# Feed-forwards in chunks of 4, 8, 6 and 4 inner tiles instead of 4, 6, 6 and 6

## The chip, the cores and the metric

The kernel runs on one core of one Trainium2 chip. A core has a matrix engine (TensorE, "PE" in the profile; its weight loads are listed apart as "PEld"), a vector engine (VectorE, "DVE"), a scalar engine (ScalarE, "ACT"), a general one (GpSimd, "POOL") and a queue engine (SyncE, "SP"), each with its own instruction stream, and DMA queues that move data between DRAM and the on-chip memory. The engines run side by side and wait for each other through semaphores. The metric is device time in microseconds for one execution; lower is better. The time of a kernel is the median of several executions.

## The reference

The model is a two-layer decoder trunk over 528 tokens (16 meta tokens and 512) of width 1024 in float32. Each layer has a feed-forward, a token mixer, and a second feed-forward, each between two RMS norms, with a residual:

```python
def swiglu(x, w_in, w_out):
    gate, up = jnp.split(x @ w_in, 2, axis=-1)
    return (jax.nn.silu(gate) * up) @ w_out

for layer in range(DEPTH):
    g = norm_gains[layer]
    h = h + 0.5 * rmsnorm(swiglu(rmsnorm(h, g[0]), w_ffn_in[layer, 0], w_ffn_out[layer, 0]), g[1])
    hn = rmsnorm(h, g[2])
    ...
    h = h + rmsnorm(mix, g[3])
    h = h + 0.5 * rmsnorm(swiglu(rmsnorm(h, g[4]), w_ffn_in[layer, 1], w_ffn_out[layer, 1]), g[5])
    if layer == N_A_LAYERS - 1:
        k_sh, v_sh = shared_kv(h, kv_norm, w_kv, cos, sin)
return h[:, N_META:]
```

The mixer of layer 0 is chunked gated linear attention, that of layer 1 sliding-window attention over keys and values that are made once between the layers. The feed-forward's inner width is 2816, that is 22 tiles of 128. All weights come from DRAM.

## The kernel before

Activations lie transposed: 128 features on the partitions, tokens along the free dimension, so a token group of 272, 256 or 512 columns is the moving side of a matmul. Each float32 product is made of three matmuls on two float32r halves, high x high, low x high and high x low (`mm3`, L428; its instructions are all recorded at L202). So every weight tile that arrives from DRAM in a `raw` buffer is split before its use: ACT copies the high half (L271 for plain weights, L291 for half-size ones) and DVE subtracts it to get the low half (L274, L292). The two halves lie in one slot of a pool of 40 `pair` tiles.

A feed-forward (`ffn`, L876) goes through its 22 inner tiles in four chunks, `FF_CHUNKS` (L24).

- Chunk 0 is plain. Gate and up products of four inner tiles, then a plain down-projection whose result Y goes to DRAM as `y_sum` (`keep=True`).
- The others use a Strassen-Winograd scheme: a block product of two by two blocks is done in seven half-size products instead of eight. The profile shows these as `a`, `c`, `d` and `e`, by the PSUM bank they go to. One `Gated` item (L1120) makes gate and up of one inner tile: seven products of 4 x 3 matmuls each, 264 columns in layer 0, 256 in layer 1. The order of an item's products on PE is "11", "s1", "s2", "12", "s3", "s4", "22", but "11" of the next item is issued ahead of the last two of this one. Two `Gated` items fill one `Step` (L1046), whose seven combinations are the right-hand operands of a half-size down-projection. `Down` items (L1181), four for each of chunks 1 and 2, multiply them with the down weights: seven products of `nk` x 3 matmuls, with `nk` = 3 steps. Their result is added to `y_sum` in DRAM by POOL's DMA (L1213).
- The `Down` items of a chunk stand after the first `Gated` item of the next chunk (`BEFORE_DOWN`, L37). The last chunk has no `Down`: its inner tiles are turned into plain hidden tiles `hid` (L1173, ACT; L1174, DVE), and a plain down-projection (`out_steps`, L775) ends the feed-forward. It adds its products to Y (L816), which has been read back from `y_sum`.

In that last plain down-projection PE runs `y_m` for the eight output tiles m over token group 0, then the same over group 1; each `y_m` is 3 matmuls for each inner tile of the last chunk. Before the last hidden tile exists, PE begins `y_0`, `y_1` and `y_2` with the earlier hidden tiles (L844 to L847), `y_0` ahead of the last item's last products, the other two behind them. Each finished Y tile is squared (ACT, L534), summed (POOL, L535) and scaled (ACT, L835). After a group's last tile, `Residual.run` (L612) makes the norm's factor: PE sums the squares over the partitions (`st_post`), DVE does ten small operations (L446 to L460) and spreads the result on a diagonal (`dg_post`, L493), PE turns it into a row for all partitions (`r_post`). Then, for each of eight tiles, DVE adds to the residual H (L626, L627) and the next phase's operand is built: its high half on ACT (L564), its low half on DVE (L565). The next phase (`x` in the profile: `l0m` is layer 0's mixer, `kv` the shared keys and values, `l1m` layer 1's mixer) runs over group 0 first. After the last feed-forward there is no next phase; for group 1 `turn` (L649) sums the squares (`st_out`), transposes H and Y and writes the output.

PE's instructions stand in the order in which the program is written out; a planned clock (`Flow`, L77) decides at which point of that order the background jobs (splits, factors, builds) issue theirs. On DVE, ACT and POOL a scheduler orders them, and each engine works through its own list in order. The number of split half-size weights in flight is limited by `set_ahead(16, RING)` with ten slots.

The DVE operations of a half-size weight pair are sums of its quarters: a pair is either `summed`, where two of the sums are made by accumulating DMAs of POOL (L350), or in `plain_sums`, where DVE makes them (L324). Down weights with 384 columns were always the second kind.

Of the kernel before, what the change touches and what calls it, by code (L numbers as in the profile page):

```python
# [16 lines left out]
P = 128  # L17
D = 1024
KD = 8
# [3 lines left out]
NFF = 22  # L23
FF_CHUNKS = [(0, 4), (4, 10), (10, 16), (16, 22)]  # L24
LAST = 16
NLAST = NFF - LAST
# [6 lines left out]
RAWS = 13  # L33
RING = 10
STEP = 1.1
CHAINS = 2
BEFORE_DOWN = 1  # L37
# [103 lines left out]
def trunk_kernel(ctx: ExitStack, tc, a, out, last_out):  # L141
# [76 lines left out]
    units, plain_sums = [], set()  # L218
    for layer in range(2):
        for f in range(2):  # L220
            for ci, (lo, hi) in enumerate(FF_CHUNKS):
                for t in range(lo, hi):
# [4 lines left out]
                    if ci > 1 and t == lo + BEFORE_DOWN - 1:  # L227
                        units += [[a["w_down"][layer, f, ci - 2, m], a["w_down"][layer, f, ci - 2, m + 1]] for m in range(0, KD, 2)]
                if lo == 0:
# [104 lines left out]
    def load_unit():  # L334
        i = len(loaded)
        asked[0] += costs[i]
        owed[i] = costs[i]
        if isinstance(units[i], list):
            g, u = units[i]
            chains[0] += 1  # L340
            m = g.shape[-1] // 2
            summed = i not in plain_sums and m == 512
            a11, a12, a21, a22 = (b[:, c : c + m] for b in (g, u) for c in (0, m))
# [25 lines left out]
        else:  # L369
            n = units[i].shape[-1]  # L370
            raws = []
            for c in range(0, n, 512):
                m = min(512, n - c)
# [502 lines left out]
    def ffn(x, groups, finish, opening=False, tail=4):  # L876
# [62 lines left out]
        plan = []  # L939
# [4 lines left out]
        for c, (lo, hi) in enumerate(FF_CHUNKS[1:]):  # L944
            for t in range(hi - lo):
                plan.append(lambda c=c, t=t: Gated(tiles, steps[c][t // 2] if c < 2 else None, t % 2))
                if c and t == BEFORE_DOWN - 1:
                    plan += [lambda c=c, q=q: Down(tiles, steps[c - 1], q) for q in range(KD // 2)]
        lo, hi = FF_CHUNKS[-1]
        hids, jobs = [], []  # L950

# [8 lines left out]
        for i in range(len(plan)):  # L960
            last = i == len(plan) - 1
            if last:
                proj = out_steps(hids, groups, x.groups, False, finish, KD, True, jobs)
                end = used[0] + NLAST + tail
            cur.body((lambda: next(proj)) if last else (lambda: None))
            nxt = None if last else begin(plan[i + 1])
            job = cur.tail(last)
            if job is not None:
                jobs.append(job)
            cur = nxt  # L970
            if i == len(plan) - 4:
                Y.fresh()
                for q in range(KD // 2):
                    pool.dma_start(Y[:, 2 * q : 2 * q + 2, kept], y_sum[:, 2 * q : 2 * q + 2, kept])
# [206 lines left out]
    class Down(Item):  # L1181
        nk = 3

        def __init__(self, tiles, steps, q):
            super().__init__(tiles)
            self.steps, self.q = steps, q
            self.y = yp.tile([P, 2, TOK], F32, tag="dn", name=f"dn{self.name}")
# [636 lines left out]
def _layout(x, meta_tokens, norm_gains, w_ffn_in, w_ffn_out, gla_w_in, gla_w_gate, gla_b_gate, gla_norm,  # L1824
# [7 lines left out]
    c["w_out"] = wo[:, :, :, :, : FF_CHUNKS[0][1]].reshape(2, 2, KD, P, FF_CHUNKS[0][1] * P)  # L1832
    c["w_down"] = np.stack([
        np.concatenate([wo[:, :, :, :, lo + i : hi : 2] for i in range(2)], axis=4) for lo, hi in FF_CHUNKS[1:3]
    ], axis=2).reshape(2, 2, 2, KD, P, 6 * P)
    c["w_last"] = (
# [66 lines left out]
```

## Time and profile before

| | |
|---|---|
| median of 3 runs | 1846.03 us (1844.55 to 1847.69) |
| the profiled execution | 1848.01 us, span 1846.2, mean granted TensorE clock 0.997 |
| PE busy | 1834.5 us (99% of the span) in 14743 matmuls |
| DVE, ACT, POOL busy | 1459.9 (79%), 1119.6 (61%), 324.0 (18%) |
| half-size gated weights, DVE low half, 128x512 | 504 at 0.69 us each |
| the same of the down weights, 128x384 | 224 at 0.55 us each |
| sums of quarters on DVE, 128x384 | 128 at 0.55 us each |
| down results added in DRAM | 32 DMAs, 8.2 to 8.6 us from issue to landing |
| DMA | 270 MB moved, mean 146 GB/s |

The profile is one execution taken by the hardware profiler. The span is the time from the first to the last instruction; what the execution took beside it is 1.8 us. Busy times of PE count overlapping matmuls once. A row of a timeline has the start, the length, the engine, the line of the program, the operation, "output <- inputs" by the program's names, shapes and the number of instructions merged; in brackets stands the idle time before it and what ended it.

### The profile page before, as it was taken

To read this page: it belongs to the slowest core of one execution; us is meant where nothing else is said; L and a number is where in the kernel's file an instruction comes from. 1 tells how busy PE (TensorE), PEld (TensorE's weight loads), DVE (VectorE), ACT (ScalarE), POOL (GpSimd) and SP (SyncE) were. 2 spreads that over 40 slices of the span, in tenths; PEclk is the share of its full clock that TensorE was granted. 3 is DMA by queue.
4 is the path that set the end of the run, shared out by engine and by line. 5 is a ranking of instruction groups with operands and counts; after the bars stand their busy time and mean duration, and the time that the engine had idled before them with its cause. 6 is when DMAs were issued, how large, how long until landed. Compare 5 with 4: busy or idle time off the path is not lost.

```text
span 1846.2 us, 38789 instructions
## 1 busy us (share of the span) xinstructions
PE 1834.5 (99%) x14743; PEld 1780.8 (96%) x14743; DVE 1459.9 (79%) x3029; ACT 1119.6 (61%) x2613; POOL 324.0 (18%) x487
## 2 busy tenths in 40 slices
PE   9999999999999999999999999999999999999998
PEld 9999999999999999999999899999987898999998
DVE  6889888666664788988878789898667678898884
ACT  6666666654446566665665566666558765666564
POOL 2210101320001411011133110112320042111122
PEclk9999999999999999999999999999999999999999
DMA  6756659421213366666853565768421226657681
GB/s 244 196 152 156 166 150 247 151 70 58 69 58 115 105 173 154 155 167 151 252 180 104 143 161 148 181 151 243 153 80 47 70 91 162 161 152 175 156 252 49
DMA packets 143371, 269.98 MB, mean 146 GB/s; under 512 B 16080, under 2 KB 36432, under 8 KB 143184
## 3 DMA queue, kind: packets, MB, share of 16 engines
q1 hardware_dynamic: 113056, 194.94, 32.8%
q0 software_dynamic: 29696, 71.97, 19.6%
q8 instruction: 115, 1.88, 0.4%
q14 instruction: 72, 0.59, 0.1%
q10 hardware_dynamic: 432, 0.59, 0.1%
HBM read 230.74 MB, written 36.18 MB: 145 GB/s over the span
## 4 chain that ended last, share of the span: by engine, by line
PE 93%; DVE 4%; ACT 2%; issue 1%; DMA 1%; DVEq 0%; SPq 0%; POOLq 0%; ACTq 0%
PE a L202 28%; PE x L202 22%; PE y L202 17%; PE c L202 13%; PE d L202 7%; PE o L202 1%; DVE w L292 1%; PE po L202 1%; DVE w_s L292 1%; ACT s L1623 1%; DVE raw L297 1%; DMA raw<-in_w_in 1%; ACT w_s L291 0%; PE pt L214 0%; PE sa L202 0%
## 5 line engine op out<-in xcount | busy, mean ns | idle before, releaser
L292 DVE TENSOR_TENSOR w_s<-raw,w_s 128x512 fp32r<-128x512 f32 (+1 forms) x416 | 264.2, 646 | 73.6 <-ACT w_s L291 69.6
L291 ACT ACTIVATE w_s<-raw 128x512 fp32r<-128x512 f32 (+1 forms) x416 | 241.0, 592 | 89.2 <-DVE raw L324 49.2
L292 DVE TENSOR_TENSOR w<-raw,w 128x512 fp32r<-128x512 f32 (+1 forms) x312 | 196.2, 645 | 4.0
L274 DVE TENSOR_TENSOR w<-raw,w 128x512 fp32r<-128x512 f32 x248 | 164.5, 695 | 37.0 <-ACT w L271 34.7
L350 POOL DMA_DIRECT2D raw<-in_w_in x112 | 103.4, 967 | 453.2 <-DVE w L292 97.1
L291 ACT ACTIVATE w<-raw 128x512 fp32r<-128x512 f32 (+1 forms) x312 | 177.7, 589 | 0.0
L297 DVE TENSOR_TENSOR raw<-raw,raw 128x512 f32<-128x512 f32 (+1 forms) x256 | 162.7, 636 | 2.2
L202 PE MATMUL x<-x_l0m,w 128*128 128x272 f32 (+1 forms) x1152 | 152.2, 289 | 0.0
L202 PEld LDWEIGHTS x<-x_l0m,w 128*128 128x128 f32 x1152 | 143.4, 188 | 2.7 <-issue 1.7
L271 ACT ACTIVATE w<-raw 128x512 fp32r<-128x512 f32 x248 | 144.1, 620 | 2.5 <-DMA raw<-in_w_in 1.2
L535 POOL TENSOR_TENSOR acc_post<-acc_post,sq_post 128x256 f32<-128x256 f32 (+1 forms) x77 | 61.7, 802 | 360.8 <-ACT sq_post L534 357.2
L202 PE MATMUL y<-hidl0f,w 128*128 128x272 f32 (+1 forms) x960 | 119.3, 285 | 0.0
L202 PEld LDWEIGHTS y<-hidl0f,w 128*128 128x128 f32 x960 | 117.9, 188 | 0.2
L202 PE MATMUL a<-zl0f_t,w_s 128*128 128x264 f32 x864 | 116.8, 284 | 0.0
L202 PE MATMUL y<-hidl1f,w 128*128 128x256 f32 (+1 forms) x768 | 114.8, 310 | 0.0
L202 PE MATMUL a<-zl1f_t,w_s 128*128 128x256 f32 x864 | 113.8, 281 | 0.0
L202 PEld LDWEIGHTS y<-hidl1f,w 128*128 128x128 f32 x768 | 104.9, 188 | 8.5
L202 PEld LDWEIGHTS a<-zl0f_t,w_s 128*128 128x128 f32 x864 | 109.9, 188 | 0.0
L202 PEld LDWEIGHTS a<-zl1f_t,w_s 128*128 128x128 f32 x864 | 107.1, 188 | 0.0
L1213 POOL DMA_DIRECT2D kept_y<-dn x32 | 36.3, 1134 | 400.5 <-DVE w_s L292 203.7
L202 PE MATMUL x<-x_l0f,w 128*128 128x256 f32 (+1 forms) x768 | 98.9, 289 | 1.5 <-ACT w L271 1.1
L202 PEld LDWEIGHTS x<-x_l0f,w 128*128 128x128 f32 x768 | 96.2, 191 | 2.2 <-ACT w L271 1.3
(568 smaller groups left out, 4118.7 us busy)
## 6 DMA issues: line engine op xcount, KB each, us to landing
raw<-in_w_in SPq DMA_DIRECT2D x408, 256.0 KB, 4.2
raw<-in_w_in POOLq DMA_DIRECT2D x112, 256.0 KB, 5.4
raw<-in_w_down SPq DMA_DIRECT2D x128, 192.0 KB, 2.4
raw<-in_w_last SPq DMA_DIRECT2D x48, 256.0 KB, 4.9
raw<-in_gla_in SPq DMA_DIRECT2D x48, 256.0 KB, 3.2
kept_y<-dn POOLq DMA_DIRECT2D x16, 528.0 KB, 8.2
raw<-in_w_out SPq DMA_DIRECT2D x32, 256.0 KB, 3.1
kept_y<-dn POOLq DMA_DIRECT2D x16, 512.0 KB, 8.6
```

Of the source, the lines that this page charges most:

```text
L202: inst = pe.matmul(o, lhs, rhs, start=start, stop=stop, skip_group_check=onto)
L271: high = act.activation(w[:, 0, :m], raw[:, :m], AF.Copy)
L274: dve.tensor_tensor(w[:, 1, :m], raw[:, :m], w[:, 0, :m].bitcast(F32), op=ALU.subtract)
L291: act.activation(w[:, 0, :m], src, AF.Copy)
L292: dve.tensor_tensor(w[:, 1, :m], src, w[:, 0, :m].bitcast(F32), op=ALU.subtract)
L297: return dve.tensor_tensor(dst, dst, src, op=ALU.add)
L350: added = pool.dma_start(r, src, accum_op=ALU.add)
L535: pool.tensor_tensor(sums[0][:, :n], sums[0][:, :n], t[:, :n], op=ALU.add)
L1213: pool.dma_start(y_sum[:, 2 * self.q : 2 * self.q + 2, o : o + 2 * n], self.y[:, :, : 2 * n], accum_op=ALU.add)
L1623: act.activation(s[:, c], s[:, c], AF.Exp, scale=rc[:, c % 2 : c % 2 + 1], bias=nm[:, c : c + 1], accum_out=den[:, c : c + 1],)
```

## The change

The inner tiles are cut differently: 4, 8, 6, 4 instead of 4, 6, 6, 6. So chunk 1 has four steps, and the first four `Down` items have `nk` = 4 (weights of 128x512 instead of 128x384); chunk 2 keeps three. The last plain down-projection has four inner tiles instead of six, so a `y_m` is 12 matmuls for each token group instead of 18. The number of `Gated` and `Down` items doesn't change. All down weights are in `plain_sums`. From the item ahead of the first `Down` on until the last of these four, the ring of split weights has eight slots instead of ten (`CLOSE_RING`). Y is read back from DRAM one item later.

```diff
-FF_CHUNKS = [(0, 4), (4, 10), (10, 16), (16, 22)]
-LAST = 16
+FF_CHUNKS = [(0, 4), (4, 12), (12, 18), (18, 22)]
+LAST = 18
 NLAST = NFF - LAST
...
 RING = 10
+CLOSE_RING = 8
...
                     if ci > 1 and t == lo + BEFORE_DOWN - 1:
-                        units += [[a["w_down"][layer, f, ci - 2, m], a["w_down"][layer, f, ci - 2, m + 1]] for m in range(0, KD, 2)]
+                        plain_sums.update(range(len(units), len(units) + KD // 2))
+                        c0, c1 = (c * P - FF_CHUNKS[1][0] * P for c in FF_CHUNKS[ci - 1])
+                        units += [[a["w_down"][layer, f, m + e, :, c0:c1] for e in range(2)] for m in range(0, KD, 2)]
...
-            summed = i not in plain_sums and m == 512
+            summed = i not in plain_sums
...
         lo, hi = FF_CHUNKS[-1]
+        wide = FF_CHUNKS[1][1] - FF_CHUNKS[1][0] + BEFORE_DOWN
...
             cur.body((lambda: next(proj)) if last else (lambda: None))
+            if i + 2 == wide:
+                set_ahead(16, CLOSE_RING)
+            elif i + 1 == wide + KD // 2:
+                set_ahead(16, RING)
...
-            if i == len(plan) - 4:
+            if i == len(plan) - 3:
                 Y.fresh()
...
     class Down(Item):
-        nk = 3
-
         def __init__(self, tiles, steps, q):
             super().__init__(tiles)
-            self.steps, self.q = steps, q
+            self.steps, self.q, self.nk = steps, q, len(steps)
```

The layout of `w_down` in DRAM is changed to fit (both chunks side by side along the columns).

Two places show what this does to the order of instructions; lines of the changed kernel are 1 to 8 higher than before (L202 becomes L203, L274 L277, L816 L819, L1163 L1171, L1174 L1182). The first is the end of the first feed-forward on PE. Ahead of these rows stands the last half-size product; `y_m_0` is output tile m over group 0, `hidl0f_n` the hidden tile of inner tile n. Before:

```order
680 L202 MATMUL y_1_0_4476<-hidl0f_16_3166,w_1_4292 128x272 x3
681 L202 MATMUL y_1_0_4476<-hidl0f_17_3734,w_1_4292 128x272 x3
682 L202 MATMUL y_1_0_4476<-hidl0f_18_3862,w_0_4313 128x272 x3
683 L202 MATMUL y_1_0_4476<-hidl0f_19_3992,w_0_4313 128x272 x3
684 L202 MATMUL y_1_0_4476<-hidl0f_20_4132,w_0_4313 128x272 x3
685 L202 MATMUL y_2_0_4519<-hidl0f_16_3166,w_1_4335 128x272 x3
686 L202 MATMUL y_2_0_4519<-hidl0f_17_3734,w_1_4335 128x272 x3
687 L202 MATMUL y_2_0_4519<-hidl0f_18_3862,w_1_4335 128x272 x3
688 L202 MATMUL y_2_0_4519<-hidl0f_19_3992,w_1_4335 128x272 x3
689 L202 MATMUL y_2_0_4519<-hidl0f_20_4132,w_0_4358 128x272 x3
690 L202 MATMUL y_0_0_4394<-hidl0f_21_4264,w_1_4292 128x272 x3
```

And changed:

```order
702 L203 MATMUL y_1_0_4562<-hidl0f_18_3522,w_1_4384 128x272 x3
703 L203 MATMUL y_1_0_4562<-hidl0f_19_4090,w_1_4384 128x272 x3
704 L203 MATMUL y_1_0_4562<-hidl0f_20_4218,w_1_4384 128x272 x3
705 L203 MATMUL y_2_0_4585<-hidl0f_18_3522,w_0_4405 128x272 x3
706 L203 MATMUL y_2_0_4585<-hidl0f_19_4090,w_0_4405 128x272 x3
707 L203 MATMUL y_2_0_4585<-hidl0f_20_4218,w_0_4405 128x272 x3
708 L203 MATMUL y_0_0_4486<-hidl0f_21_4356,w_0_4361 128x272 x3
```

Between the last half-size product and the first use of the last hidden tile, `hidl0f_21`, stand 18 matmuls instead of 30. On DVE the making of that tile's low half reads, changed:

```order
530 L1172 TENSOR_TENSOR c_4357<-c_4357 128x264
531 L1171 TENSOR_TENSOR c_4357<-a_1_1169,c_4357 128x264
532 L277 TENSOR_TENSOR w_1_4566<-raw_512_4422,w_1_4566 128x512
533 L277 TENSOR_TENSOR w_0_4569<-raw_0_4465,w_0_4569 128x512
534 L277 TENSOR_TENSOR w_1_4572<-raw_512_4467,w_1_4572 128x512
535 L1182 TENSOR_SCALAR hidl0f_21_4356<-c_4357,hidl0f_21_4356 128x528
```

Three weight splits stand between the last operation on the gated product and the low half; before, the same three stood ahead of the L1163 operation (now L1171).

The second place is the phase after the first feed-forward, on DVE, around the factor of group 1 (`dg_post_l0m`). Before, from the last build of group 0's operand on:

```order
588 L627 TENSOR_TENSOR H_3_4474<-t_l0m_4997,H_3_4474 128x272
589 L565 TENSOR_SCALAR x_l0m_5000<-H_3_4474,vec,x_l0m_5000 128x272
590 L1262 TENSOR_TENSOR lr<-lr,vec 128x256
591 L446 TENSOR_SCALAR av_post_l0m_5036<-st_post_l0m_5031 128x2
592 L449 TENSOR_SCALAR yv_post_l0m_5037<-av_post_l0m_5036 128x2
593 L452 TENSOR_TENSOR zv_post_l0m_5038<-yv_post_l0m_5037 128x2
594 L453 TENSOR_TENSOR zv_post_l0m_5038<-zv_post_l0m_5038,av_post_l0m_5036 128x2
```

Changed, from the same first operation of the root on:

```order
584 L449 TENSOR_SCALAR av_post_l0m_4984<-st_post_l0m_4979 128x2
585 L630 TENSOR_TENSOR H_2_4558<-t_l0m_5000,H_2_4558 128x272
586 L452 TENSOR_SCALAR yv_post_l0m_4985<-av_post_l0m_4984 128x2
587 L629 TENSOR_TENSOR t_l0m_5021<-Y_3_4283,r_post_l0m_4833 128x272
588 L455 TENSOR_TENSOR zv_post_l0m_4986<-yv_post_l0m_4985 128x2
589 L629 TENSOR_TENSOR t_l0m_5042<-Y_3_4283,r_post_l0m_4833 128x272
590 L456 TENSOR_TENSOR zv_post_l0m_4986<-zv_post_l0m_4986,av_post_l0m_4984 128x2
591 L568 TENSOR_SCALAR x_l0m_5003<-H_2_4558,vec,x_l0m_5003 128x272
592 L457 TENSOR_SCALAR wv_post_l0m_4987<-zv_post_l0m_4986 128x2
593 L630 TENSOR_TENSOR H_3_4560<-t_l0m_5021,H_3_4560 128x272
594 L458 TENSOR_TENSOR wv_post_l0m_4987<-wv_post_l0m_4987,zv_post_l0m_4986 128x2
595 L630 TENSOR_TENSOR H_3_4560<-t_l0m_5042,H_3_4560 128x272
```

Two more of the low halves (L568) and the root's last operations follow, then `dg_post`. So the builds of the last three tiles of group 0, which were done before the root of group 1 began, are now mixed with it. On PE the matmul that waits for it, `r_post_l0m`, stands behind 60 matmuls of the `x` phase, before behind 57 and the `st_l0m`.

More of the change, by code (lines that the diff above doesn't have):

```diff
@@ L1832, in _layout @@
     c["w_out"] = wo[:, :, :, :, : FF_CHUNKS[0][1]].reshape(2, 2, KD, P, FF_CHUNKS[0][1] * P)
-    c["w_down"] = np.stack([
-        np.concatenate([wo[:, :, :, :, lo + i : hi : 2] for i in range(2)], axis=4) for lo, hi in FF_CHUNKS[1:3]
-    ], axis=2).reshape(2, 2, 2, KD, P, 6 * P)
+    c["w_down"] = np.concatenate(
+        [wo[:, :, :, :, lo + i : hi : 2] for lo, hi in FF_CHUNKS[1:3] for i in range(2)], axis=4
+    ).reshape(2, 2, KD, P, (LAST - FF_CHUNKS[1][0]) * P)
     c["w_last"] = (
```

## The prediction

> **What bounds the kernel now.** I read the page first: busy time and the chain that ended last.
>
> ```profile
> PE 1834.5 (99%) x14743; PEld 1780.8 (96%) x14743; DVE 1459.9 (79%) x3029; ACT 1119.6 (61%) x2613; POOL 324.0 (18%) x487
> ...
> PE 93%; DVE 4%; ACT 2%; issue 1%; DMA 1%; DVEq 0%; SPq 0%; POOLq 0%; ACTq 0%
> ```
>
> TensorE (PE) runs for 99% of the span, and the chain is PE for 93%. So a matmul that is taken away is worth its start-to-start time, and a wait of PE costs its length. The view of waits, for PE and then for its weight loads, shows how little PE waits; the columns are the sum in us, the number, the longest:
>
> ```profile
> PE r_post_kv L202 <- DVE dg_post_kv L493: 0.5, 1, 0.5
> PEld a L202 <- ACT dn L1199: 1.3, 5, 0.3
> ```
>
> Such small sums mean that the covers are only just long enough. Below 0.2% (3.7 us) a measurement of this kernel can't be told from no change, and the whole question is whether covers that become shorter give back what the matmuls save.
>
> **What is removed and added.** In each of the four feed-forwards the last plain down-projection loses two of its six inner tiles: 8 outputs x 2 groups x 2 tiles x 3 = 96 matmuls fewer. The first half-size down-projection gets a fourth operand pair: 4 items x 7 products x 3 = 84 matmuls more. From the chain in order of time (start, length, engine, what, count) and from the timeline (start, length, ...):
>
> ```profile
> 330.63 20.14 PE y L202 x162
> ...
> 355.31 9.55 PE y L202 x81
> ```
>
> ```profile
> 97.25 1.62 PE L202 MATMUL d<-zl0f,w 128*128 128x264 f32 x12
> ...
> 117.67 1.63 PE L202 MATMUL d<-zl0f,w 128*128 128x264 f32 x12
> ```
>
> One y matmul takes 20.14/162 = 0.1243 us (272 columns) or 9.55/81 = 0.1179 (256). Half-size items repeat every 84 matmuls, and the two d rows are two items apart: 20.42/168 = 0.1215 (264 columns). Layer 0, each feed-forward: 48 x 0.1243 + 48 x 0.1179 - 84 x 0.1215 = 1.42 saved. In layer 1 both kinds have 256 columns: 12 x 0.1179 = 1.41. Together **-5.7**. The waits for dn (1.3 in all) belong to both down-projections: a d product of 12 matmuls (1.46) instead of 9 covers the copy of the first one; I take **-0.5**, between 0 and -1.3.
>
> **Shorter cover for the last hidden tile.** After the last half-size product PE begins y_1 and y_2 (30 matmuls now, 18 changed), then needs the last hidden tile, whose low half DVE makes (L1174). Timeline, layer 0, first feed-forward:
>
> ```profile
> 330.47 6.71 PE L202 MATMUL y<-hidl0f,w 128*128 128x272 f32 x52
> 330.67 1.90 DVE L274 TENSOR_TENSOR w<-raw,w 128x512 fp32r<-128x512 f32 x3
> 332.48 0.42 DVE L1163 TENSOR_TENSOR c<-a,c 128x264 f32<-128x264 f32 x1
> 333.62 0.71 DVE L1174 SCALAR_TENSOR_TENSOR hidl0f<-c,hidl0f 128x528 fp32r<-128x528 f32 x1 [0.71 <-ACT hidl0f L1173]
> ```
>
> The low half lands at 334.33. PE gets there at 330.47 + 30 x 0.1243 + 0.25 (two matmuls with the high half) = 334.45: no wait, with 0.1 to spare. In the changed order three weight splits still lie on DVE ahead of the low half, now behind the L1163 operation. PE's last product ends 0.16 after the y start (the chain's first y piece begins at 330.63, above), so 0.16 + 0.42 + 1.90 + 0.71, and 0.16 for the signal (an estimate from dg_post to r_post below), is 3.35 after it; PE arrives at 18 x 0.1243 + 0.25 = 2.49. Wait 0.86, about 0.8 in layer 1's first feed-forward; the fourth has no splits there, and its low half is in time. **+2.5**; between 0 (the splits ran earlier) and +4.3 (one more split, 0.63, ahead in each).
>
> **Shorter cover for the next operand.** This is the largest cost. The plain down-projection runs token group 0, then group 1. While PE does group 1 (144 matmuls, 96 changed), DVE adds up Y, and from group 0's factor on builds the eight tiles of the next operand. Then the next phase (x) uses them, and inside it PE needs group 1's factor: st_post, ten small DVE operations, dg_post, then r_post. Group 1 ends at 364.70 here:
>
> ```profile
> 364.70 4.31 PE L202 MATMUL x<-x_l0m,w 128*128 128x272 f32 x33
> 368.85 0.95 PE L202 MATMUL st_post_l0m<-ones,acc_post 128*128 128x1 f32 x8
> 369.66 1.75 PE L202 MATMUL x<-x_l0m,w 128*128 128x272 f32 x12
> 371.25 0.60 PE L202 MATMUL st_l0m<-ones,acc_l0m 128*68 128x1 f32 x8
> 371.70 1.75 PE L202 MATMUL x<-x_l0m,w 128*128 128x272 f32 x12
> 373.30 0.59 PE L202 MATMUL r_post_l0m<-dg_post_l0m,ones 128*128 128x256 f32 x2
> ...
> 357.63 0.44 DVE L626 TENSOR_TENSOR t_l0m<-Y,r_post_l0m 128x272 f32<-128x272 f32 x1
> 358.11 0.44 DVE L627 TENSOR_TENSOR H<-t_l0m,H 128x272 f32<-128x272 f32 x1
> 358.46 0.49 DVE L565 SCALAR_TENSOR_TENSOR x_l0m<-H,vec,x_l0m 128x272 fp32r<-128x272 f32 x1
> 358.87 0.42 DVE L816 TENSOR_TENSOR Y<-y,Y 128x256 f32<-128x256 f32 x1
> ...
> 367.93 0.50 DVE L565 SCALAR_TENSOR_TENSOR x_l0m<-H,vec,x_l0m 128x272 fp32r<-128x272 f32 x1 [0.65 <-ACT x_l0m L564]
> ...
> 369.83 0.16 DVE L446 TENSOR_SCALAR av_post_l0m<-st_post_l0m 128x2 f32<-128x2 f32 x1 [1.07 <-PE st_post_l0m L202]
> ...
> 371.80 0.42 DVE L493 TENSOR_TENSOR dg_post_l0m<-ident,yv_post_l0m 128x256 f32<-128x256 f32 x1
> ```
>
> Now DVE is done with the eight builds at 368.43, before st_post can be read (369.83), so the root runs alone: ten operations in 1.97, dg_post at 372.22, and PE arrives 1.1 later. Changed, PE enters x 48 x 0.1179 = 5.7 earlier and the builds don't move, since they hang on group 0's factor. In the changed order three builds are still unfinished when the root begins, woven between its operations, and dg_post stands behind all of them. From the start of x: st_post at +4.15 (33 matmuls, as now), the first root operation 0.98 later (369.83 - 368.85), then 3 x L627, 2 x L626 and 3 x L565 with start-to-start times of 0.35, 0.48 and 0.41 (the rows from 357.63), so 3.2, the root 2.0, dg_post 0.42, and 0.16 to PE: +10.9. PE reaches r_post after 60 x matmuls and the st_post: now it takes 8.60 (373.30 - 364.70) with 57 and the st_l0m (0.45); so 8.60 - 0.45 + 3 x 0.1243 = +8.5. It waits **2.4**, and all of x behind r_post waits with it. Without those builds ahead dg_post would be there at +7.7, so 0 is the lower bound. If ACT's copy ahead of each build (the 0.65 gap above) slows the three builds, the wait grows to some 3.5.
>
> The same order, operation by operation, stands ahead of kv (second feed-forward): again 2.4. Ahead of l1m (third) DVE has one L627 and one L565 less before dg_post, and 71 x matmuls stand before r_post:
>
> ```profile
> 1331.06 4.06 PE L202 MATMUL x<-x_l1m,w 128*128 128x256 f32 x33
> ...
> 1340.54 0.59 PE L202 MATMUL r_post_l1m<-dg_post_l1m,ones 128*128 128x256 f32 x2
> ```
>
> There PE takes 9.48 now with 69 matmuls and a st_l1m like the one above, so 9.48 - 0.45 + 2 x 0.1179 = 9.3; dg_post lands at 10.9 - 0.76 = 10.1: 0.8. Sum **+5.6**, between 0 and +9.
>
> **The end of the program.** The last st_out waits for POOL's sum of output 6, under cover of output 7's matmuls:
>
> ```profile
> 1832.25 4.39 PE L202 MATMUL y<-hidl1f,w 128*128 128x256 f32 x36
> 1836.71 0.61 PE L202 MATMUL st_out<-ones,acc_post 128*128 128x1 f32 x4
> 1835.93 0.73 POOL L535 TENSOR_TENSOR acc_post<-acc_post,sq_post 128x256 f32<-128x256 f32 x1 [1.78 <-ACT sq_post L534]
> ```
>
> POOL ends at 1836.66, PE's matmuls at 1836.64: no slack. Output 7 shrinks from 18 to 12 matmuls, 0.7 less cover: **+0.7** (0 to 1.4).
>
> **What I cost at nothing.** Eight slots of split weights instead of ten around the first half-size down-projection: one product takes 12 x 0.1215 = 1.46 and DVE's share of a split 0.63 (1.90/3 above), so eight slots are still seven products, some ten microseconds, of lead. If that cover is gone, PE waits for a product or two, 1.5 to 2.9 in each feed-forward. Wider splits (512 columns instead of 384 in the first down-projection, two weight units fewer at the end) lie on DVE, busy 79%, and ACT, 61%, beside PE's products. Y comes back from DRAM one item later, which leaves the last gated items (10.2 each) and the begins before its first use.
>
> **Sum**: -5.7 - 0.5 + 2.5 + 5.6 + 0.7 = **+2.6**. The profiled execution took 1848.01 (span 1846.2), 2.0 above the median of 1846.03; there it would be 1850.6, and on the median **1848.6**. Own range of this case: 1845.5 to 1852.5.
>
> **Rivals.**
> (a) *The waits stay hidden.* The order on DVE leaves room: if the builds run faster than I reckon, they are done when the root begins, and the splits when the low half does. For it: each of my waits is a difference of two long sums, and today's trace hides all of them. Against it: DVE works in order, and the three builds stand ahead of dg_post. Only the saving is left, with the end's 0.7 at most: 1846.0 - 6.2 + (0 to 3) = 1840 to 1843, faster.
> (b) *The ring of eight starves PE.* Place: the last items before and the items of the first half-size down-projection, where L291 and L292 must deliver a part each 1.46. It decides once a part's split ends less than a product ahead of its use. With 1.5 to 2.9 in each of four feed-forwards on top of my sum: 1854.6 to 1860, slower. Against it: no half-size weight is among the things that PE waits on now.
> (c) *The clock falls after a wait.* The windows view (stretch, length, busy time of each engine, granted clock, DMA) shows it once, near the start, where PE was busy for 0.79 of 2 us, and the next four ran at a mean clock of 0.57:
>
> ```profile
> 6.00:8.00 2.00, 0.79 (x4) 0.38 (x3) 0.86 (x2) 1.05 (x2) 0.00 (x0) 1.00 1.01 357
> 8.00:12.00 4.00, 3.75 (x17) 3.75 (x18) 3.74 (x9) 3.87 (x10) 0.00 (x0) 0.57 1.07 390
> ```
>
> A wait of 2.4 leaves PE idle longer than that stretch did. 0.43 of 4 us is 1.7 lost; behind two or three r_post waits that is +3.4 to +5.1: 1852.0 to 1853.7, slower. [...]
> (d) *The chains end sooner by half*, and waits and saving cancel: 1846.
>
> **How the numbers follow.** Forecast 0.50: its range reaches past +3.7 and my waits are bounded further above than below, so 0.24 same and 0.26 slower. (a) 0.25: 0.24 faster, 0.01 same. (b) 0.12 and (c) 0.08 slower. (d) 0.05 same. Together faster 0.24, same 0.30, slower 0.46. The range reaches down to 1841 into (a) and up to 1856, which holds (c) and the lower edge of (b).
>
> **What would show it.** Right: about 48 matmuls fewer; waits of PE for dg_post_l0m and dg_post_kv of 2 to 3 us, for dg_post_l1m about 1, for the low half of the last hidden tile 0.8 in three feed-forwards, st_out for POOL 0.7. Wrong: no such waits (then faster, (a)); PE waiting on w_s or w of L291 and L292 around the first half-size down-projection (b); a granted clock below 1 behind r_post (c).

## The result and the profile after

The changed kernel takes 1856.08 us (median of 6 runs, 1853.68 to 1859.41); the kernel before, run beside it, 1846.76 (6 runs, 1844.55 to 1847.69). The ratio is 1.0054 [1.0041, 1.0067]: slower by half a per cent. That is 0.08 above the upper end of the range and 7.5 above the predicted 1848.6. The profiled execution took 1856.21 with a span of 1854.4, so it is 8.2 longer than the profiled one of before (1846.2).

Busy times and the chain of waits of the changed kernel, from its page of the profile:

```profile
PE 1831.7 (99%) x14695; PEld 1775.3 (96%) x14695; DVE 1485.8 (80%) x3033; ACT 1129.7 (61%) x2605; POOL 322.4 (17%) x487
...
PE 84%; DVE 8%; ACT 3%; DMA 2%; issue 2%; SPq 0%; POOL 0%; POOLq 0%; DVEq 0%; ACTq 0%
```

There are 48 matmuls fewer and PE is busy for 2.8 us less, as the change intends. But DVE now has 8% of the chain that ends last instead of 4%, and PE 84% instead of 93%. What PE waits for there stands in the view of waits (sum, number, longest, in us), with the weight loads last:

```profile
PE r_post_kv L203 <- DVE dg_post_kv L496: 4.0, 2, 2.7
PE r_post_l0m L203 <- DVE dg_post_l0m L496: 2.9, 1, 2.9
...
PE y L203 <- DVE hidl0f L1182: 0.9, 2, 0.4
...
PE r_post_l1m L203 <- DVE dg_post_l1m L496: 0.6, 1, 0.6
...
PE y L203 <- DVE hidl1f L1182: 0.6, 1, 0.6
PE a L203 <- ACT htl1f L1151: 0.5, 1, 0.5
PE st_out L203 <- POOL acc_post L538: 0.5, 1, 0.5
...
PEld a L203 <- ACT dn L1205: 1.2, 4, 0.3
```

Of these, only a wait of 0.5 for dg_post_kv and 1.3 for dn were there before. To see where the time comes from along the program, compare the starts of the same instruction in both timelines:

| landmark on PE | before | after | difference | of the stretch |
|---|---|---|---|---|
| r_l0m of group 1 (first feed-forward and the phase behind it are done) | 398.36 | 402.13 | +3.8 | +3.8 |
| r_kv of group 1 (second feed-forward) | 999.29 | 1006.26 | +7.0 | +3.2 |
| first `sa` of the attention (third feed-forward) | 1367.20 | 1374.59 | +7.4 | +0.4 |
| first `st_out` (fourth feed-forward) | 1836.71 | 1843.53 | +6.8 | -0.6 |
| end of the span | 1846.2 | 1854.4 | +8.2 | +1.4 |

A stretch with a feed-forward and without any new wait would stand at -1.4. None does, and the two feed-forwards of layer 0 lose the most. The attention of layer 1, which lies in the stretch to `st_out`, is the same in both: PE runs the same order there, and from the first `sa` to the first half-size product of the fourth feed-forward it takes 194.96 before and 195.04 after.

The stretch of the first: timeline of the changed kernel around group 1's factor, PE first, then DVE (start, length, engine, what; idle time before it in brackets):

```profile
368.89 3.62 PE L203 MATMUL x<-x_l0m,w 128*128 128x272 f32 x27
375.46 1.22 PE L203 MATMUL r_post_l0m<-dg_post_l0m,ones 128*128 128x256 f32 x2 [2.95 <-DVE dg_post_l0m L496]
376.12 5.76 PE L203 MATMUL x<-x_l0m,w 128*128 128x272 f32 x35
...
369.27 0.15 DVE L449 TENSOR_SCALAR av_post_l0m<-st_post_l0m 128x2 f32<-128x2 f32 x1
...
374.06 1.01 DVE L568 SCALAR_TENSOR_TENSOR x_l0m<-H,vec,x_l0m 128x272 fp32r<-128x272 f32 x1
374.99 0.41 DVE L496 TENSOR_TENSOR dg_post_l0m<-ident,yv_post_l0m 128x256 f32<-128x256 f32 x1
```

The root of group 1 begins at 369.27 and its dg_post ends at 375.40, 6.1 later: the builds of group 0's last three tiles lie between, as forecast. PE has nothing to do for 2.95. Then something more happens. The 35 matmuls behind the wait take 5.59 to the next instruction (381.71), 0.160 each instead of 0.124. The windows view of the same stretch says why; its third number from the end is the granted clock:

```profile
374.00:376.00 2.00, 0.54 (x1) 0.50 (x2) 2.00 (x4) 0.79 (x2) 0.76 (x1) 0.74 0.00 0
376.00:378.00 2.00, 2.00 (x9) 1.86 (x8) 1.29 (x4) 0.00 (x0) 0.00 (x0) 0.50 0.45 119
378.00:380.00 2.00, 2.00 (x17) 2.00 (x16) 1.93 (x6) 1.63 (x4) 0.07 (x1) 0.90 0.40 142
```

The clock is halved from about 375.0 to 378.4. At the start of r_post the kernel is 2.16 behind the kernel before, at r_l0m 3.77: the halved clock costs 1.6 on top of the wait.

The end of the program, DVE and SyncE of the changed kernel:

```profile
1847.09 2.73 DVE L688 SCALAR_TENSOR_TENSOR t_out<-turn_out,half_out,h_out 128x512 f32<-128x512 f32 x4
1849.73 0.69 DVE L642 TENSOR_TENSOR t_out<-Y,r_post_out 128x512 f32<-128x512 f32 x1
1850.45 0.69 DVE L643 TENSOR_TENSOR H<-t_out,H 128x512 f32<-128x512 f32 x1
...
1851.17 0.38 SPq L644 DMA_DIRECT2D out<-H  x1
```

Before, the L685 row (now L688) is the last thing that DVE does. Now the fourth of the four pieces in which group 0's output is stored (`store`, one piece for each planned unit of time) stands behind it, because the planned time until the end has become shorter by output tiles that are a third smaller. Its DMA is issued at 1851.17, and the span ends later by it: from the first st_out to the end it was 9.5 before and is 10.9 now.

### The profile page after: what moved, and what is told of

Same layout as the page of the kernel before. It is cut to its first block, busy times and chain, and to the rows that moved or that the text cites. A ratio compares the mean times of both kernels' runs of the same rounds, so it can differ in the third digit from the quotient of the medians.

```text
span 1854.4 us, 38705 instructions
## 1 busy us (share of the span) xinstructions
PE 1831.7 (99%) x14695; PEld 1775.3 (96%) x14695; DVE 1485.8 (80%) x3033; ACT 1129.7 (61%) x2605; POOL 322.4 (17%) x487
## 4 chain that ended last, share of the span: by engine, by line
PE 84%; DVE 8%; ACT 3%; DMA 2%; issue 2%; SPq 0%; POOL 0%; POOLq 0%; DVEq 0%; ACTq 0%
PE a L203 26%; PE x L203 20%; PE y L203 13%; PE c L203 13%; PE d L203 6%; DMA raw<-in_w_in 2%; DVE w L295 2%; DVE raw L300 1%; DVE w_s L295 1%; PE o L203 1%; ACT s L1629 1%; ACT w_s L294 1%; PE po L203 1%; DMA H<-in_h 1%; DVE w L277 0%
## 5 line engine op out<-in xcount | busy, mean ns | idle before, releaser
L295 DVE TENSOR_TENSOR w_s<-raw,w_s 128x512 fp32r<-128x512 f32 (+1 forms) x416 | 272.2, 667 | 79.6 <-ACT w_s L294 76.0
L294 ACT ACTIVATE w_s<-raw 128x512 fp32r<-128x512 f32 (+1 forms) x416 | 247.8, 609 | 100.7 <-DVE raw L300 51.2
L295 DVE TENSOR_TENSOR w<-raw,w 128x512 fp32r<-128x512 f32 (+1 forms) x312 | 202.1, 666 | 6.0 <-ACT w L294 2.1
L277 DVE TENSOR_TENSOR w<-raw,w 128x512 fp32r<-128x512 f32 x232 | 155.5, 701 | 30.5 <-ACT w L274 28.4
L300 DVE TENSOR_TENSOR raw<-raw,raw 128x512 f32<-128x512 f32 (+1 forms) x256 | 169.2, 661 | 2.1
L203 PE MATMUL x<-x_l0m,w 128*128 128x272 f32 (+1 forms) x1152 | 153.2, 290 | 0.0
L203 PEld LDWEIGHTS x<-x_l0m,w 128*128 128x128 f32 x1152 | 144.4, 190 | 2.8 <-issue 1.7
L274 ACT ACTIVATE w<-raw 128x512 fp32r<-128x512 f32 x232 | 134.3, 620 | 0.9 <-DMA raw<-in_w_in 0.7
L203 PE MATMUL a<-zl0f_t,w_s 128*128 128x264 f32 x864 | 116.9, 284 | 0.0
L203 PE MATMUL a<-zl1f_t,w_s 128*128 128x256 f32 x864 | 114.0, 281 | 0.5 <-ACT htl1f L1151 0.5
L203 PEld LDWEIGHTS a<-zl0f_t,w_s 128*128 128x128 f32 x864 | 109.8, 188 | 0.0
L203 PEld LDWEIGHTS a<-zl1f_t,w_s 128*128 128x128 f32 x864 | 107.2, 188 | 0.7 <-ACT htl1f L1151 0.7
L203 PE MATMUL x<-x_l0f,w 128*128 128x256 f32 (+1 forms) x768 | 98.1, 287 | 1.4 <-DVE w L277 0.9
L203 PEld LDWEIGHTS x<-x_l0f,w 128*128 128x128 f32 x768 | 94.8, 188 | 2.8 <-DVE w L277 1.5
L203 PE MATMUL y<-hidl0f,w 128*128 128x256 f32 (+1 forms) x768 | 96.2, 285 | 0.9 <-DVE hidl0f L1182 0.9
L203 PEld LDWEIGHTS y<-hidl0f,w 128*128 128x128 f32 x768 | 94.4, 188 | 1.5 <-DVE hidl0f L1182 1.3
L203 PE MATMUL y<-hidl1f,w 128*128 128x256 f32 (+1 forms) x576 | 92.5, 320 | 0.6 <-DVE hidl1f L1182 0.6
L203 PE MATMUL x<-x_l1f,w 128*128 128x256 f32 (+1 forms) x576 | 92.8, 320 | 0.0
## 6 DMA issues: line engine op xcount, KB each, us to landing
raw<-in_w_down SPq DMA_DIRECT2D x64, 192.0 KB, 2.4
```

Of the source, the lines that this page charges most:

```text
L203: inst = pe.matmul(o, lhs, rhs, start=start, stop=stop, skip_group_check=onto)
L274: high = act.activation(w[:, 0, :m], raw[:, :m], AF.Copy)
L277: dve.tensor_tensor(w[:, 1, :m], raw[:, :m], w[:, 0, :m].bitcast(F32), op=ALU.subtract)
L294: act.activation(w[:, 0, :m], src, AF.Copy)
L295: dve.tensor_tensor(w[:, 1, :m], src, w[:, 0, :m].bitcast(F32), op=ALU.subtract)
L300: return dve.tensor_tensor(dst, dst, src, op=ALU.add)
```

## Experiments

The theory after the result: the loss is the waits of PE at the four feed-forward ends, r_post of group 1 above all, plus what hangs on them (the clock) and the last store. The rivals: the ring of eight starves PE along the feed-forwards; or the waits are only where the loss shows, and without them it turns up elsewhere.

**Ten slots again (rival: the ring).**

```diff
-CLOSE_RING = 8
+CLOSE_RING = 10
```

> The changed kernel, with ten slots for split weights around the first half-size down-projection in place of eight. Theory A (eight slots cost nothing): the same time within its spread, and each feed-forward's stretch from its start to the last half-size product within 0.2. Rival B (the ring starves PE): 4 or more less.

Measured: 1855.81 (1853.31 to 1859.13, 4 runs), ratio to before 1.0056 [1.0043, 1.007]. PE reaches the last half-size product of the first feed-forward 9.25 later than before with ten slots and 9.29 later with eight. 84 matmuls more there at 0.1215 less six fewer of y_0 at 0.1243 make 9.46, so there is no starving in either. The second and third feed-forward give 9.46 and 9.28 with eight slots, 9.45 and 9.24 with ten (first to last half-size product, against before). The ring is free, and the rival falls.

**Later r_post of group 1.** The planned clock is told that group 1's factor takes longer, so that PE gets more x matmuls ahead of r_post. No other line is changed, but the planned clock places everything behind it anew.

```diff
+LATE = 3.0
...
     nxt, fin = into("l0m", 0, 1, True, lambda k: gain(0, 2, k), L0, (1, 1))
+    fin.factors[1] = LATE
...
     nxt.more = BUSY
+    fin.factors[1] = LATE
...
-        fin.factors[1] = SLACK
+        fin.factors[1] = SLACK + 1.0
```

> The changed kernel, with PE's r_post of token group 1 issued 3 us later in its own order ahead of l0m and kv, and 1 us later ahead of l1m; nothing else. Theory A (the loss is PE waiting for dg_post behind the operand builds on DVE, and the clock that falls after such a wait): the waits of 2.9, 2.7 and 0.6 are gone and no clock drop follows them; the time falls by 6 to 10 us from the changed kernel's 1856.1, to 1846 to 1850. Group 1's builds begin later, which may cost up to 2 of it. Rival B (the loss lies in the half-size items, in the ring of eight and the wider splits, and the waits only stand where PE would have waited for something else): the time falls by less than 2, and other waits take their place.

Measured: 1848.56 (1848.14 to 1850.03, 11 runs), ratio 1.0013 [1.0004, 1.0022]: 7.5 of the 9.3 are back. That is the time of theory A, but not all of it is theory A's doing. The table takes the profiled executions apart by stretches of PE and gives each as its difference to the kernel before; "FF" is the first half-size product of a feed-forward.

| stretch on PE | changed | later r_post |
|---|---|---|
| start to the second FF (with l0m) | +3.6 | +0.8 |
| on to the third FF (with kv) | +3.3 | +3.6 |
| on to the first `sa` (with l1m) | +0.5 | +0.7 |
| on to the fourth FF (the attention) | +0.1 | -3.8 |
| on to the first `st_out` | -0.7 | -0.7 |
| on to the end | +1.4 | +1.3 |

At l0m 2.9 are back: there the wait, with its drop of the clock, is the cause and doesn't merely mark the loss, and a wait of 0.6 for a build comes in its place. At kv nothing is back, since the waits move to other places. And 3.8 are won in the attention, where the changed kernel had lost nothing. The new delays have moved the order on PE there. Changed kernel, then this one:

```profile
1389.85 2.34 PE L203 MATMUL x<-x_l1m,w 128*128 128x512 f32 x9
...
1396.50 1.07 PE L203 MATMUL turn<-q,sel 128*32 128x512 f32 x8
...
1387.45 0.94 PE L204 MATMUL x<-x_l1m,w 128*128 128x512 f32 x3
1388.32 1.06 PE L204 MATMUL turn<-q,sel 128*32 128x512 f32 x6
```

Two things make up the 3.8. The granted clock is halved in the attention for 6.8 us in some executions, for 3.4 or not at all in others, each 3.4 costing 1.5: with the old order the attention takes 195.0 (here, 6.8), 193.5 (with one more output tile begun, 3.4) and 192.0 (with ten slots, none). The other 2.3 is the order: of the four kernels with later r_post, one takes 192.6 with 6.8 us of halved clock, and three, this one among them, take 191.2 with 3.4. Which of the three delays moved the order was not separated, and the kernel before was not given it. So the hit in the time is in part luck, and rival B is right in that other waits come in at kv. The waits of this kernel there:

```profile
PE r_kv L204 <- POOL dg_kv L497: 1.9, 1, 1.9
PE r_post_kv L204 <- DVE dg_post_kv L497: 1.3, 1, 1.3
```

r_kv is the next factor, made on POOL. The timeline of this kernel, POOL and then DVE:

```profile
999.39 4.75 POOL L456 TENSOR_TENSOR zv_kv<-yv_kv 128x2 f32<-128x2 f32 x1
1004.22 0.20 POOL L457 TENSOR_TENSOR zv_kv<-zv_kv,av_kv 128x2 f32<-128x2 f32 x1
...
999.19 4.89 DVE L278 TENSOR_TENSOR w<-raw,w 128x512 fp32r<-128x512 f32 x8
```

A two-column operation that took 0.19 in the kernel before (L452 there) lasts 4.75 here, as long as DVE's unbroken run of eight splits beside it (4.89) and not as one of them (0.61); the next one, right behind the run, takes 0.20. In the kernel before, eight operations of the same chain ran beside an unbroken run of eight splits as well (992.67 to 997.57), and took 0.50 to 0.54 each. So in both kernels POOL's operations were longer beside such a run, and the order of the jobs decides which of them fall into it; why this one lasted for all of it, no run settles.

**A wait alone, in the kernel before.** If a wait costs more than its length, it must do so without any of the change. DVE computes the dg_post of group 1 ahead of l0m ten or twenty times more, with the same result.

```diff
+REPEAT = 10
...
-        made = eng.tensor_tensor(
...
+        for _ in range(1 + REPEAT * (name == "post_l0m1")):
+            made = eng.tensor_tensor(
```

> The kernel before, with dg_post of token group 1 ahead of l0m computed ten times more on DVE (some 3.5 to 4.2 us more, 1.1 of it hidden), so that PE waits 2.4 to 3.1 there and nowhere else. Theory A (a wait of this length can halve the clock for the 3.4 us behind it): +2.4 to +3.1, and in some executions 1.7 more, with a granted clock of 0.50 behind r_post where it happens. Without the clock: +2.4 to +3.1 in all executions, clock 1.00 behind it.

> The same with twenty more computations, so that PE waits some 6 to 7 us. [...] If waits have no part in the clock, 6 to 7 and clock 1.00 behind it.

Measured with ten: 1853.05 (1850.28 to 1853.47, 5 runs), ratio 1.0033 [1.002, 1.0045]. PE waits 3.4. r_post starts 3.46 later than before, r_l0m 4.86 later, so 1.4 comes from behind the wait, where the windows view shows:

```profile
376.00:378.00 2.00, 1.24 (x3) 1.06 (x4) 0.67 (x2) 0.00 (x0) 1.31 (x3) 0.54 0.04 8
378.00:380.00 2.00, 2.00 (x12) 2.00 (x12) 1.88 (x5) 0.95 (x3) 0.00 (x0) 0.60 0.00 0
```

The five runs fall into two groups: 1850.28 and 1851.10 at a mean clock of 0.999, 1853.05 to 1853.47 at 0.997. That doesn't show that the wait costs the clock in some executions only: the 16 runs of the kernel before that were taken beside it go from 1844.67 to 1848.45, with the mean clock falling from 1.000 to 0.998 as well, and the drop in the attention alone costs 0, 1.5 or 3.0.

The wait also costs a little more than its idle time. r_post starts 3.46 later, and up to the wait this execution is 0.11 ahead of that of before, so PE is held for 3.57, while the timeline counts 3.42 idle. The profile counts from the end of the last matmul (0.28 long), but the next would have started 0.12 after that one's start. So this wait of PE cost some 0.16 on top; for other waits the same is an estimate.

With twenty: 1854.49 (1853.91 to 1855.12, 4 runs), ratio 1.0045 [1.0031, 1.0059]. Timeline and windows of that kernel:

```profile
381.69 1.22 PE L203 MATMUL r_post_l0m<-dg_post_l0m,ones 128*128 128x256 f32 x2 [8.32 <-DVE dg_post_l0m L495]
...
378.00:379.00 1.00, 0.00 (x0) 0.00 (x0) 0.93 (x3) 0.00 (x0) 0.00 (x0) 0.76 0.00 0
...
385.00:386.00 1.00, 1.00 (x8) 1.00 (x8) 1.00 (x4) 0.60 (x2) 0.32 (x1) 0.82 0.00 0
```

The clock falls while PE still waits and stays halved until 385.4. r_l0m is 10.17 later: 8.39 at r_post and 1.78 behind it. A wait of 8.3 pays the clock once, about as much as one of 3.4. The span ends only 6.95 later, since this execution has no drop in the attention.

**The last store earlier.** The fourth piece is planned 0.8 after the third instead of 1.0.

```diff
-                yield 1.0
+                yield 0.8 if k == 4 else 1.0
```

> The changed kernel, with the last pair of group 0's stores issued 0.8 in place of 1.0 of planned time after the third, which puts it on DVE behind output 6's sum and ahead of the final root. If the end is lost to that pair behind the final outputs (two operations of 0.69 and their DMA): st_out as in the changed kernel, the stretch from st_out to the end 1.0 shorter (1.4 less some 0.4 that the root now starts later). If the end is set by something else, the stretch stays as it is.

Measured: 1854.60 (1854.46 to 1856.15, 4 runs), ratio 1.0051 [1.0037, 1.0064]. In the profile the first st_out starts at 1843.20 and the span ends at 1852.7, 9.5 later, as before the change. So the last store was worth 1.4. The interval of the ratio alone could not have shown this: it overlaps that of the changed kernel.

**One more output tile begun.** PE begins a further `y_m` ahead of the last hidden tile, as cover for its low half.

```diff
-            for m, g in order[1 : (2 if order[1][1][1] == SEQ else 3) + keep]:
+            for m, g in order[1 : (2 if order[1][1][1] == SEQ else 3) + (keep or nh == NLAST)]:
```

> The changed kernel, with one more output tile begun behind the last half-size product: 27 matmuls of cover for the last hidden tile in place of 18, at all four feed-forwards' ends. If the short cover is the loss there: the waits for hidl0f and hidl1f (0.9 and 0.6) are gone, some 1.5 less at st_post of the last group, of which part may come back as a longer wait for r_post_kv of group 0. If the waits would only move: no difference at r_post of group 0 in any feed-forward.

Measured: 1855.57 (1855.24 to 1855.75, 4 runs), ratio 1.0054 [1.004, 1.0067]: no difference from the changed kernel that these runs can show. The waits for hidl0f and hidl1f are gone, and at group 0's st_post_l0m it is 0.8 ahead of the changed kernel. But at kv the saved time is waited out at the next factor:

```profile
PE r_post_kv L203 <- DVE dg_post_kv L496: 4.8, 2, 2.7
```

4.8 instead of 4.0: PE came earlier to a factor that did not. The clock, too, falls elsewhere. At l0m PE waits 2.9 as in the changed kernel, but no drop follows, and twice at kv one does, although the second wait there is the same 2.73 that had none in the changed kernel. The windows show what goes with it. Up to the last products, all drops in these profiles last 3.41 us or twice that, and within one execution they begin whole multiples of 3.41 apart (here at 960.38, 977.45 and 1410.94). So cut the time into stretches of 3.41 that end where a drop begins. Changed kernel, l0m and then kv:

```profile
371.57:374.98 3.41, 0.94 (x8) 0.72 (x6) 3.23 (x10) 2.61 (x6) 1.74 (x3) 1.00 0.00 0
374.98:378.39 3.41, 2.93 (x11) 2.75 (x12) 2.67 (x7) 0.28 (x1) 0.00 (x0) 0.50 0.29 77
...
972.26:975.68 3.42, 2.44 (x20) 2.22 (x18) 3.23 (x11) 1.96 (x7) 1.42 (x2) 1.00 0.00 0
975.68:979.09 3.41, 1.67 (x11) 1.61 (x12) 3.31 (x9) 0.84 (x4) 0.98 (x2) 1.00 0.01 2
979.09:982.50 3.41, 3.41 (x31) 3.41 (x30) 3.34 (x9) 3.13 (x8) 0.73 (x1) 1.00 0.40 154
```

With one more output tile begun, the same two places:

```profile
369.85:373.26 3.41, 1.85 (x15) 1.63 (x13) 3.24 (x13) 2.00 (x6) 1.71 (x3) 1.00 0.00 0
373.26:376.68 3.42, 2.04 (x14) 1.99 (x15) 3.23 (x7) 0.71 (x2) 0.69 (x1) 1.00 0.11 25
...
974.03:977.45 3.42, 0.69 (x5) 0.48 (x4) 3.20 (x9) 2.27 (x6) 1.52 (x2) 1.00 0.01 2
```

Where nearly all of the wait falls into one stretch, PE is busy for 0.94 or 0.69 of it and the next runs at half the clock. Where the border cuts the wait in two, PE is busy for 1.67 to 2.44 in each part, and no drop follows. The border lies elsewhere in each execution.

**All at once, the store's pace too fast.** The later r_post and the further begin, and all four pieces of the store 0.6 apart (`yield 0.6`).

> The same, and two more repairs: one more output tile is begun with the earlier hidden tiles behind the last half-size product (27 matmuls of cover in place of 18), and the planned pace of group 0's last stores at the program's end is 0.6 in place of 1.0, so that the last pair no longer stands behind the final outputs on DVE. Theory A: a further 1.5 (waits for the last hidden tile) and 1.4 (two DVE operations of 0.69 at the very end) less than with the late r_post alone, so 1843 to 1847, about 2 us under the kernel before at best: the saving of 5.7 less the 0.5 of st_out, the 1.3 of r_post_kv of group 0 and small ones. Rival B: not below 1852.

Measured: 1852.41 (1851.75 to 1853.21, 6 runs), ratio 1.0032 [1.002, 1.0044], worse than the later r_post alone. Its waits and its timeline on DVE:

```profile
PE st_out L204 <- POOL acc_post L539: 3.4, 1, 3.4
...
1835.60 1.29 DVE L643 TENSOR_TENSOR t_out<-Y,r_post_out 128x512 f32<-128x512 f32 x2
1836.80 1.28 DVE L644 TENSOR_TENSOR H<-t_out,H 128x512 f32<-128x512 f32 x2
1838.00 0.42 DVE L820 TENSOR_TENSOR Y<-y,Y 128x256 f32<-128x256 f32 x1
```

The store no longer comes last; it comes ahead of the last sum of Y (L820), which DVE could have made at 1836.44, when PE's last product ends. ACT's square, POOL's sum and st_out stand behind it. The clock falls here, too (0.50 in the window 1842 to 1844). A miss, but one that prices the other side: one piece too late costs 1.4, two pieces too early make PE wait 3.4.

**Each wait with its own delay.** Two versions: later r_post, the further begin, the last store at 0.8, and at kv other delays for the three factors in turn. The second one:

```diff
     nxt, fin = into("l0m", 0, 1, True, lambda k: gain(0, 2, k), L0, (1, 1))
+    fin.factors[1] = 2.7
...
-    nxt.more = BUSY
+    nxt.more = BUSY + 1.0
+    fin.factors = [1.8, 2.0]
...
-        fin.factors[1] = SLACK
+        fin.factors[1] = SLACK + 1.0
```

The first has 3.0 at l0m and `[1.2, 3.0]` at kv.

> The late r_post of group 1, with kv's r_post of group 0 1.2 later and the norm's r_kv 1.0 later as well, one more output tile begun, and the last stores as in the run before. Theory A: from the 1848.6 of the late r_post alone, some 1.3 less at r_post_kv, 1 to 1.9 at r_kv, 1.5 at the last hidden tiles, 1.0 at the end: 1843 to 1845.5, under the kernel before (1846.5). If waits only move from one place to the next: 1847 or more.

> The kernel with all repairs once more, with the delays sized by the waits that were left: r_post of group 1 2.7 later ahead of l0m (3.0 before) and 2.0 ahead of kv (3.0), r_post_kv of group 0 1.8 later (1.2). Theory A: the 1.15 that PE waited for x_kv's first build of group 1 and most of the 0.7 for dg_post_kv are gone, and nothing takes their place: 1843 to 1844, some 0.1% under the kernel before. If the waits only move: 1845 as in the run before.

Measured: the first 1845.03 (1844.03 to 1846.95, 11 runs), ratio 0.9994 [0.9985, 1.0003]; the second 1844.04 (1842.61 to 1845.19, 11 runs), ratio 0.9987 [0.9978, 0.9996], the fastest of all kernels here, with a span of 1842.2 in its profile. Its waits, and r_post at l0m in its timeline:

```profile
PE x L203 <- ACT x_kv L567: 0.8, 1, 0.8
...
PE r_post_kv L203 <- DVE dg_post_kv L496: 0.6, 2, 0.4
...
368.32 6.62 PE L203 MATMUL x<-x_l0m,w 128*128 128x272 f32 x51
374.91 0.70 PE L203 MATMUL r_post_l0m<-dg_post_l0m,ones 128*128 128x256 f32 x2
```

84 x matmuls (33 and 51) now stand ahead of r_post instead of 60, and it waits for nothing. The first st_out comes 4.0 earlier than before the change and the span ends 4.0 earlier. By the stretches of the table under "Later r_post of group 1" the differences are -1.1, +1.5, +0.1, -3.8, -0.8 and 0.0. So 3.8 of the 4.0 lie in the attention: 2.3 by its new order and 1.5 because this execution has one stretch of halved clock there and that of before had two. Neither has to do with the matmuls that were removed. Outside of the attention the kernel is 0.2 faster than before, where the changed one is 8.1 slower. So with these delays the loss is made good, 4.7 of it at l0m, 1.8 at kv and 1.4 at the end, and the waits and the last store are shown as its cause there. But of the 5.7 that the matmuls save next to nothing is seen: at kv, above all, the kernel is still 1.5 behind. The kernel before has hardly a wait at its factors to take away, but it was not run with these delays, and the new order of its attention might make it as fast.

## Why the prediction was right or wrong

**Right:** the sign, for the forecast reason. The matmuls saved what they should: 48 fewer, and the stretch up to the last half-size product agrees with the sum to 0.2 in the first three feed-forwards (the fourth has a wait of 0.5 for a copy in it). The largest term, r_post of group 1, was 5.6 and measured 6.3: 2.95, 2.73 and 0.6 where 2.4, 2.4 and 0.8 were forecast. st_out waited 0.5 (0.7). The ring of eight cost nothing (0). That gives rivals (a) and (b) up: the waits are there, and the ring is not among them.

**Mis-sized:** the last hidden tile, +2.5 forecast, 0.43 + 0.43 + 0.56 = 1.4 measured. The step that failed is the sum of DVE's lengths. Timeline of the changed kernel:

```profile
339.74 2.68 PE L203 MATMUL y<-hidl0f,w 128*128 128x272 f32 x20
342.85 3.40 PE L203 MATMUL y<-hidl0f,w 128*128 128x272 f32 x25 [0.43 <-DVE hidl0f L1182]
...
339.94 0.43 DVE L1171 TENSOR_TENSOR c<-a,c 128x264 f32<-128x264 f32 x1
340.29 1.89 DVE L277 TENSOR_TENSOR w<-raw,w 128x512 fp32r<-128x512 f32 x3
342.10 0.70 DVE L1182 SCALAR_TENSOR_TENSOR hidl0f<-c,hidl0f 128x528 fp32r<-128x528 f32 x1
```

The second and third DVE row start 0.08 before the one ahead of them ends, and the signal to PE took 0.05 where 0.16 was taken, a length that no row shows (in the kernel before, too, it is 0.05 from the end of dg_post_kv at 951.98 to r_post_kv at 952.03). So from the start of y to the first use it took 3.11, not 3.35. PE's 20 matmuls took the 2.49 that were forecast up to where the next could start; that the profile sees the last one end at 2.68 makes the idle time 0.43 and not 0.62. For r_post the same prediction used start-to-start times and came within 0.7. The other one is dn: its waits went from 1.3 to 1.2, not to 0.8.

**Left out of the sum:** five things, in order of size.

1. The clock. It was rival (c), at a chance of 0.08, and it happened: 1.6 in the profiled run, by the drop behind r_post at l0m (the drop in the attention is there before, too). Two things were wrong in how it was put. It was a rival to the sum, though a wait can cost both, and the one of 2.95 did; and its chance, the author's estimate, was set low against the prediction's own row, where the clock fell to 0.57 behind a stretch with PE busy for 0.79 of 2 us. The runs side with the row: waits of 2.95 (here) and 2.73 (with the further begin) are followed by a halved clock, with PE busy for 0.94 and 0.69 of the 3.41 us ahead. The six runs differ by the clock as well (1853.68 at a mean of 0.999, 1858.49 and 1859.41 at 0.995), but the mean doesn't say where: the drop in the attention is part of it.
2. The last store, +1.4. The prediction read the end of the program on PE and POOL only. On DVE the order of the changed kernel had the fourth piece behind the last L688; it could have been seen there.
3. What a wait costs beyond its idle time: some 0.16, by the one wait of the experiment with a wait alone. Taken for each of the eight new waits (three for r_post of group 1, three for hidden tiles, st_out and the copy below) that is an estimate of +1.3.
4. r_post of group 0 at kv waits 1.27 instead of 0.54, +0.7: the time from its st_post is 5.57 instead of 4.79. The prediction looked at group 1's factors alone, though this one was the only r_post that PE already waited for. What lengthened it was not followed.
5. A product `a` waits 0.5 for ACT's copy (L1151) in one of the Gated items that are now in a half-size chunk.

**The ledger** of the profiled difference: -5.7 matmuls, -0.1 dn, +1.4 hidden tile, +6.3 r_post of group 1, +0.7 r_post of group 0, +0.5 st_out, +0.5 copy, +1.6 clock, +1.4 store: +6.6 of the measured +8.2. The 0.16 estimated for each new wait make it +7.9; the rest lies in small pieces that were not followed. The medians differ by more, 9.3, because the profiled execution of before was 1.3 above its median, while that of after was at its median.

The steps that failed, in the prediction's terms: "a wait of PE costs its length", where the wait of 2.95 at l0m cost 1.6 of clock and, by the estimate above, 0.16 more; and the end of the program, costed at +0.7 for st_out alone, where the last store adds 1.4. With the clock once and the store in it, the sum would have been +2.6 + 1.6 + 1.4 = +5.6, or 1851.6 on the median. The rest of the miss is the small waits of the list, the 0.7 by which r_post of group 1 was too small and the 0.4 of the dn waits that stayed, less the 1.1 by which the hidden tile was too large.

## What to carry to other kernels

Where an engine is busy for 99% of the span, work that is taken off it is also cover that is taken off every chain beside it: list what lies beside the removed work at each boundary, read the order of every engine there up to the last DMA, and re-time these chains in the same change. Here the change alone is 0.5% slower, and with a handful of planned delays set anew it is level with the kernel before, apart from an attention that these delays speed up by the way. A saving ahead of a late factor is only waited out at the factor, so the last wait of a chain has to go first. Price a wait of TensorE of 2 to 3 us at its length and, as a chance, a drop of the clock, which cost 1.4 to 1.8 here. And when a repair wins time, ask in which stretch: an edit to a planned clock moves everything behind it.

## What the hardware showed

- The granted clock falls to 0.50 behind waits of 2.1 to 8.3 us, and not behind each of them: no drop follows the 2.9 at l0m with one more output tile begun. In the changed kernel it begins 2.5 us after PE's last matmul (372.51 to 374.98), in the kernel with the wait of 8.3 it begins 5.2 after it (373.36 to 378.52). It lasts 3.4 or 6.8 us. At l0m it cost 1.4 and 1.6, each time in 3.4 us, and 1.8 in 6.8 us, of which PE still waited for the first 3.2. What goes with it is how much PE does within one of the stretches of 3.41 us above. Around the waits for r_post and st_out in the profiles here, a drop followed each of ten stretches in which PE was busy for 0 to 1.31 us, and none of those of 1.67, 1.85 and 2.04 in the windows above. In the attention, with many short matmuls, it falls at 1.72 of 3.41 in the kernel before, at 1.71 in the changed one and at some 2.5 in the last kernel with its own delays, and at the start of the kernel before (the prediction's row) at 1.95, so PE's busy time is not the whole of it. In the attention of the kernel before it looks so:

```profile
1402.00:1408.00 6.00, 6.00 (x30) 4.69 (x29) 4.46 (x15) 3.56 (x13) 0.00 (x0) 0.51 0.56 178
```

- With later r_post, one of POOL's 128x2 operations lasted 4.75 beside eight splits on DVE (4.89), the next 0.20 right behind them; in the kernel before, such operations took 0.50 to 0.54 beside eight splits (4.90).
- DVE's 128x2 operations, 0.16 each, took 0.6 to 0.7 in places of the changed kernel's mixed root, and the last L568 there 1.01 instead of 0.49. What held them was not settled.
